# The squares for the last layer's MLP norms in the buffers of the MLP's inner products, and the decode step as a stream of its own beside the first stage

## The chip, the cores and the metric

The kernel runs on one core of one Trainium2 chip. The metric is the device time of one execution in microseconds (us); smaller is better. Times come in runs of a few executions each, of which the median is given.

## The reference, cut to what matters

One inference step of a hybrid decoder with two layers, in float32: 1024 prompt tokens with 16 learned tokens ahead of them, and 8 decode tokens that carry their own states. Width 1024, MLP width 4096. Layer 0 mixes tokens by a convolution; layer 1, the one that matters here, by RWKV-7 time mixing. For the decode tokens that is one step of a recurrence over a 64 x 64 state per head:

```python
def _wkv7_step(S, inp):
    r_t, w_t, k_t, v_t, kk_t, a_t = inp
    sa = jnp.einsum('bhvk,bhk->bhv', S, -kk_t)
    S = (S * w_t[:, :, None, :] + sa[..., None] * (kk_t * a_t)[:, :, None, :]
         + v_t[..., None] * k_t[:, :, None, :])
    y = jnp.einsum('bhvk,bhk->bhv', S, r_t)
    return S, y
...
    yn = ((y - mu) * lax.rsqrt(var + GN_EPS)).reshape(B, T, D_MODEL)
    yn = yn * gn_g.astype(f32) + gn_b.astype(f32)
    bonus = (jnp.sum(r * k * r_k.astype(f32), axis=-1, keepdims=True) * v).reshape(B, T, D_MODEL)
    out = ((yn + bonus).astype(h.dtype) * g) @ w_o
    return out, h[:, -1], S_final.astype(S0.dtype)

def _sqrelu_mlp(h, w_in, w_out):
    return jnp.square(jax.nn.relu(h @ w_in)) @ w_out
...
        h = h + out
        h = h + _sqrelu_mlp(_rmsnorm(h, norm_mlp[i]), w_mlp_in[i], w_mlp_out[i])
```

## The kernel before, in words

Activations lie with the 1024 features on 8 tiles of 128 partitions and the tokens along the free side. A matrix product in float32 is made of three fast passes: weights and activations are each split into a high part and a remainder (`_hi`/`_lo`, `_h`/`_l`), and lines L187, L188 and L189 of `mm3` add high*high, low*high and high*low in PSUM. ScalarE (ACT) writes the high parts, GpSimd (POOL) the weights' remainders in four pieces each (L162), VectorE (DVE) most of the activations' remainders.

The program has three parts: layer 0; the inputs of the time mixing, in four groups of tokens; and the last part, with which this case deals. It takes the tokens in three groups of 328, 352 and 352 (`G2`). For each group `mixer_out` loads the residual `h` (L1484) and the gated mixer output `z`, tile by tile (`zr`, L1488), splits it (`z_h`, `z_l`), multiplies it with `w_o` (`ps_oo`), adds the product to `h` on DVE (L1492), and hands each finished tile to `add`. `add` comes from `square_sums`: ACT squares the tile (L242) and POOL and DVE add the squares of even and odd tiles up (L253); a matmul with a constant (`st_m`, L231) then sums over the partitions for the norm's denominator. `mlp_in` scales `h` into `m_h` and `m_l` (L269, L270), and `mlp` multiplies by `w_in` (`ps_in`), squares, splits into `hh` and `hl` of the pool `hidp` (two buffers of each), and multiplies by `w_out` (`out`), whose product DVE adds to `h` (L340). The first group has an MLP of its own, the first stage; groups two and three share one.

Other work runs beside the first stage, in generators that `filler` advances after each half product and the like: `fill()` is called `points` times in all, and a stream with total `n` is advanced until what it yielded reaches its share of `n`. The streams are:

- `until`: the rest of the prompt's recurrence in chunks of 64 tokens. Its matmuls are small: `A` (128 x 256), then 64 x 64 (`W`, `U`, `S`, `Y`) and 32 x 32 (`gg`, `po`). Four chunks at a time need `inverses`, 30 steps of two DVE instructions each (`tt`, `ni`; L1168, L1169).
- `decode_step`: the recurrence for the decode tokens. Four transposes (`pdd`) go through DRAM (`d_dec`) by DMAs that ACT issues, come back as `dq`, and then 16 rounds of nine DVE instructions each (L1390 to L1398) with a load and a store of `Sdec` on SyncE (SP). It yields 82 in all.
- `norm_gate`: group norm, gate and bonus of up to 128 tokens at a time, in two halves (`ey`, `eq`, `ems`, `ebv`, `egt`, `ez`, and transposes `yn` on TensorE), for the second and third group. It waits by `after` until the recurrence has reached its tokens.

The order of the instructions on each engine is set when the program is built: a scheduler that goes by modelled times takes them by priority, which is the order in which the generators emit them. On the chip each engine runs its list in that order and waits by semaphores. DMAs go out through SP and ACT, over eight semaphore lanes in turn; a DMA is held back until the one before it on its lane is done. Pools lie one above the other in memory, and a tile is written once the earlier users of its bytes are done.

In the kernel before, the squares have a tag of their own with three buffers, so that the fourth square waits for the first to be added:

```python
return square_sums(n, f"m1{g}", lambda k: cur["tmp"].tile([P, cur["n"]], F32, name=f"sq{g}_{k}", tag="sq", bufs=3)[:, :n],
                   (nc.gpsimd, nc.vector))
```

and the decode step stands ahead of the norm gates in one stream of 262.15.

Of the kernel before, what the change touches and what calls it, by code (L numbers as in the profile page):

```python
# [8 lines left out]
F32 = mybir.dt.float32  # L9
# [7 lines left out]
P = 128  # L17
D = 1024
KT = D // P
# [4 lines left out]
NP_TOK = META + SEQ  # L24
# [14 lines left out]
GN = [(lo + i, min(128, n - i)) for lo, n in G2 for i in range(0, n, 128)]  # L39
GN_OF = [[i for i, (lo, n) in enumerate(GN) if a <= lo < a + w] for a, w in G2]  # L40
# [8 lines left out]
def hybrid_step(tc, x_prompt, x_sample, state_conv, state_shift, state_wkv, meta_tokens,  # L49
# [8 lines left out]
    nc = tc.nc  # L58
    ctx = ExitStack()
    with ctx:  # L60
# [48 lines left out]
        for name, ap in vecs:  # L109
            n = ap.shape[0]  # L110
# [11 lines left out]
        cur = {}  # L122
# [151 lines left out]
        def ranked(offset, gen):  # L274

            it = iter(gen)
            while True:
                with tc.high_priority(offset=offset):
                    try:
                        wait = next(it)  # L280
                    except StopIteration:
                        return
                yield wait
# [85 lines left out]
        with ExitStack() as l0:  # L369
# [16 lines left out]
            h = {}  # L386
# [292 lines left out]
            hidp = pool(l0, "hidp0", 2)  # L679
# [463 lines left out]
            carry["tail"] = tail  # L1143


        st = {"done": -1, "ready": -1, "credit": 0.0}
        for name, shape in (("sv", [P, KT, 2, HS]), ("uv", [P, KT, 2, HS])):
            st[name] = wk.tile(shape, F32, name=name)
        for q in range(2):
# [196 lines left out]
        NG = 0  # L1346
# [14 lines left out]
        def decode_step():  # L1361

            with ExitStack() as s:
                dk = pool(s, "dk", 1)
                for q in range(4):
                    pt = bank(f"pdd{q}", "x")
                    for i in range(2):
                        nc.tensor.transpose(pt[:6 * DEC, i * P:(i + 1) * P],
                                            ddec[:, 2 * q + i].rearrange("p i b -> p (i b)"), ident)
                    dst = tt(f"dst{q}", "t2")[:6 * DEC, :256]  # L1370
                    nc.scalar.copy(dst, pt[:6 * DEC, :256])
                    nc.scalar.dma_start(d_dec.rearrange("i b d -> (i b) d")[:, q * 256:(q + 1) * 256], dst)
                    yield 3
                dq = dk.tile([P, 6, HS], F32, name="dq")
                nc.scalar.dma_start(dq, d_dec.rearrange("i b (h c) -> (b h) i c", c=HS))
                yield 6
                sa = dk.tile([P, HS], F32, name="sa")
                yd = dk.tile([P, HS], F32, name="yd")
                HV = HS // 16
                s_in = state_wkv[0].rearrange("b h v k -> (b h) v k")  # L1380
                s_out = o_wkv_sample[0].rearrange("b h v k -> (b h) v k")
                rows = lambda t: t[:, :HV * HS].rearrange("p (v k) -> p v k", k=HS)
                for hv in range(HS // HV):
                    vs = slice(hv * HV, (hv + 1) * HV)
                    S = rows(cur["ey"].tile([P, 4 * P], F32, name=f"Sdec{hv}", tag="ey"))
                    t4 = rows(cur["eq"].tile([P, 4 * P], F32, name=f"t4{hv}", tag="eq"))
                    nc.sync.dma_start(S, s_in[:, vs, :])
                    overv = lambda i: dq[:, i:i + 1, :].broadcast_to([P, HV, HS])
                    overk = lambda t: t.unsqueeze(2).broadcast_to([P, HV, HS])
                    nc.vector.tensor_mul(t4, S, overv(2))  # L1390
                    nc.vector.tensor_reduce(sa[:, vs], t4, axis=AX.X, op=ALU.add)
                    nc.vector.tensor_mul(S, S, overv(0))
                    nc.vector.tensor_mul(t4, overk(sa[:, vs]), overv(3))
                    nc.vector.tensor_add(S, S, t4)
                    nc.vector.tensor_mul(t4, overk(dq[:, 5, vs]), overv(1))
                    nc.vector.tensor_add(S, S, t4)
                    nc.vector.tensor_mul(t4, S, overv(4))
                    nc.vector.tensor_reduce(yd[:, vs], t4, axis=AX.X, op=ALU.add)  # L1398
                    nc.sync.dma_start(s_out[:, vs, :], S)
                    yield 4  # L1400
                nc.scalar.dma_start(d_y[NP_TOK:].rearrange("b (h c) -> (b h) c", c=HS), yd)

        def norm_gate(i):

            lo, n = GN[i]
            KH, NH = KT // 2, KT
            for hf in range(2):
                ps_ = slice(hf * KH, (hf + 1) * KH)
                y, bv, gt, sq = (cur[tag].tile([P, KH * P], F32, name=f"{tag}{i}_{hf}", tag=tag) for tag in ("ey", "ebv", "egt", "eq"))
                nc.sync.dma_start(y[:n], d_y[lo:lo + n, hf * KH * P:(hf + 1) * KH * P])  # L1410
                yield 3
                heads = lambda t: t[:n].rearrange("t (h v) -> t h v", v=HS)
                ms = cur["eq"].tile([P, 2, NH], F32, name=f"ems{i}_{hf}", tag="ems")
                over = lambda j: ms[:n, j].unsqueeze(2).broadcast_to([n, NH, HS])
                nc.vector.tensor_reduce(ms[:n, 0], heads(y), axis=AX.X, op=ALU.add)
                nc.vector.scalar_tensor_tensor(heads(y), over(0), -1.0 / HS, heads(y), op0=ALU.mult, op1=ALU.add)
                nc.scalar.activation(sq[:n], y[:n], AF.Square)
                yield 2
                fm = lambda t: t[:, :KH * n].rearrange("p (k t) -> p k t", k=KH)
                for t, src in ((bv, d_bv), (gt, d_g)):  # L1420
                    nc.sync.dma_start(fm(t), src[:, ps_, lo:lo + n])
                nc.vector.tensor_reduce(ms[:n, 1], heads(sq), axis=AX.X, op=ALU.add)
                nc.scalar.activation(ms[:n, 1], ms[:n, 1], AF.Sqrt, scale=1.0 / HS, bias=eps_t[:n, 2:3])
                nc.vector.reciprocal(ms[:n, 1], ms[:n, 1])
                nc.vector.tensor_mul(heads(y), heads(y), over(1))
                yield 2.5
                pt = bank(f"yn{i}_{hf}", "w")
                for k in range(KH):
                    nc.tensor.transpose(pt[:, k * n:(k + 1) * n], y[:n, k * P:(k + 1) * P], ident[:n, :n])
                z = cur["eq"].tile([P, KH * P], F32, name=f"ez{i}_{hf}", tag="eq")  # L1430
                for k in range(KH):
                    p = hf * KH + k
                    nc.scalar.activation(z[:, k * n:(k + 1) * n], pt[:, k * n:(k + 1) * n], AF.Identity, scale=vec("gn_g", p), bias=vec("gn_b", p))
                w = KH * n
                nc.vector.tensor_add(z[:, :w], z[:, :w], bv[:, :w])
                nc.vector.tensor_mul(z[:, :w], z[:, :w], gt[:, :w])
                nc.sync.dma_start(d_z[:, ps_, lo:lo + n], fm(z))
                yield 2.5


        NEED = [min(-(-(lo + n - META) // HS), NCH - 1) for lo, n in GN]

        def after(last, gen):
            while st["done"] < last:
                yield 1
            yield from gen

        def norm_gates(gs):
            return ranked(NG, chain.from_iterable(after(NEED[g], norm_gate(g)) for g in gs))
        ng0 = norm_gates(GN_OF[0])  # L1450
        PACE = [0, 1.7, 1.7, 0.98]

# [17 lines left out]
        with ExitStack() as l1:  # L1470
# [4 lines left out]
            hidp = pool(l1, "hidp1", 2)  # L1475
            open_ep(l1, 2, "f")
            hl = {}

            NGA, NGB, FA, FB = 262.15, 45.48, 1.57, 40

            def mixer_out(g, residp, actp, fill, add):
                lo, n = G2[g]
# [61 lines left out]
                        wait = next(rec)  # L1544
                    yield wait

            def sums_of(g):
                n = G2[g][1]
                return square_sums(n, f"m1{g}", lambda k: cur["tmp"].tile([P, cur["n"]], F32, name=f"sq{g}_{k}", tag="sq", bufs=3)[:, :n],
                                   (nc.gpsimd, nc.vector))  # L1550

            def group(g, actp, hidp, sums):
                n = G2[g][1]
# [4 lines left out]
            ng2 = norm_gates(GN_OF[2])  # L1558
            fill, rest = filler(2 * KT + MLP_POINTS,
                                ([until(NCH - 1)], FA * CHUNK_WAIT * (NCH - 1 - st["done"])),  # L1560
                                ([decode_step(), norm_gates(GN_OF[1]), ng2], NGA))
            add, sums = sums_of(0)
            mixer_out(0, residp, actp, fill, add)
            mlp(1, [group(0, actp, hidp, sums)], 2, nc.gpsimd, nc.vector, fill)
            for _ in rest:
# [4 lines left out]
            right = dict(side="right")  # L1570
            residp2, actp2, hidp2 = pool(l1, "resid2", 2, **right), pool(l1, "actp2", 1, **right), pool(l1, "hidp2", 2, **right)
            fill, rest = filler(2 * KT, ([ng2], NGB))
            add, sums = sums_of(1)
            mixer_out(1, residp2, actp, fill, add)
            for _ in rest:
                pass
# [1 line left out]
                nc.scalar.dma_start(o_conv_sample[0, q, 0:CB - 1, :], state_conv[0, q, 1:CB, :])  # L1578
            g1 = group(1, actp, hidp, sums)
            fill, rest = filler(2 * KT + MLP2_POINTS, ([ranked(FN, final(0))], FB))  # L1580
            add, sums = sums_of(2)
            mixer_out(2, residp2, actp2, fill, add)
            end = []

# [40 lines left out]
```

## Time and profile before

| | |
|---|---|
| time, median of 3 runs (lowest to highest) | 2852.09 us (2852.02 to 2855.66) |
| the profiled execution: its time, its span | 2859.05 us, 2857.3 us |
| mean granted TensorE clock | 0.961 |
| busy share: TensorE (PE), weight load (PEld), DVE, ACT, POOL | 94%, 90%, 69%, 47%, 60% |
| last part of the program, us from the span's start | about 1856 to the end |
| its first inner product (`ps_in`) | 1916.33 us |

In the views PE is TensorE's matmuls and PEld its weight loads. A row of the timeline has the start in us, the duration in us, the engine, the line, the operation, what it writes and reads, the shapes, and in brackets the idle time before it with what ended that. A row of the waits names who waited for whom, with the sum in us, how often, and the longest. A row of the windows has, for each stretch, the busy us of each engine with the number of instructions, the granted clock as a share of full speed, the DMA engines' busy share and GB/s. A float32 matmul that is not split (`A`, `S`, `Y` and the others of the recurrence) is two records in the trace for one instruction.

### The profile page before, as it was taken

The numbers are of one execution on the slowest core, as the hardware profiler recorded it, in microseconds if no ns is written. First come the engines' busy times: TensorE is split into PE (matmuls) and PEld (weight loads), VectorE is DVE, ScalarE is ACT, GpSimd is POOL, SyncE is SP. The second block draws the span as 40 slices with busy tenths as digits, with TensorE's granted clock in tenths as the row PEclk, the third lists the DMA queues.
The fourth block names the chain that finished last, engine by engine and source line by source line (L and its number), as shares of the span: only waits on it lengthen the run. The fifth ranks groups of instructions, "written<-read, shape, count | busy, mean of one in ns | idle before, by whom it ended". The sixth has DMA issues, their size and how long they took to land. (4 is left out here: it accounts for less than half of the span.)

```text
span 2857.3 us, 54445 instructions
## 1 busy us (share of the span) xinstructions
PE 2677.4 (94%) x20554; PEld 2557.9 (90%) x20554; DVE 1958.0 (69%) x3726; ACT 1345.6 (47%) x2510; POOL 1703.4 (60%) x2295
## 2 busy tenths in 40 slices
PE   8999999999999899878788899979999999999998
PEld 7989999999999898867787788778889999999998
DVE  5999999995455545478896895689656764443444
ACT  5545444543454334565666857634445552222223
POOL 6676877887788775444543554646448783333332
PEclk9999999999999999988899999989999999999999
DMA  6662544454444642777777968856557742222211
GB/s 179 172 184 85 159 135 133 133 179 140 136 129 148 176 138 91 215 194 198 202 215 208 241 165 198 234 156 159 128 161 213 205 128 85 70 72 67 67 60 41
DMA packets 659285, 428.34 MB, mean 150 GB/s; under 512 B 126840, under 2 KB 609208, under 8 KB 659022
## 3 DMA queue, kind: packets, MB, share of 16 engines
q1 hardware_dynamic: 652780, 421.93, 52.6%
q8 instruction: 162, 2.65, 0.4%
q10 hardware_dynamic: 6018, 2.89, 0.4%
q14 instruction: 101, 0.83, 0.1%
q0 software_dynamic: 224, 0.03, 0.0%
HBM read 353.03 MB, written 72.66 MB: 149 GB/s over the span
## 5 line engine op out<-in xcount | busy, mean ns | idle before, releaser
L162 POOL TENSOR_TENSOR wo_lo<-wo_raw,wo_hi 128x256 fp32r<-128x256 f32 x736 | 561.5, 795 | 300.3 <-ACT wo_hi L157 265.5
L162 POOL TENSOR_TENSOR wi_lo<-wi_raw,wi_hi 128x256 fp32r<-128x256 f32 x640 | 490.4, 797 | 275.5 <-ACT wi_hi L157 264.1
L187 PE MATMUL out<-hh,wo_hi 128*128 128x352 f32 (+2 forms) x1536 | 503.5, 328 | 20.1 <-DVE h L340 10.6
L340 DVE TENSOR_TENSOR h<-h,out 128x352 f32<-128x352 f32 (+2 forms) x768 | 386.3, 510 | 197.8 <-PE out L189 196.9
L187 PE MATMUL ps_in<-m_h,wi_hi 128*128 128x352 f32 (+2 forms) x1536 | 497.4, 324 | 12.2 <-ACT m_h L269 11.5
L189 PE MATMUL out<-hl,wo_hi 128*128 128x352 f32 (+2 forms) x1536 | 496.0, 325 | 4.0 <-DVE hl L141 4.0
L188 PE MATMUL out<-hh,wo_lo 128*128 128x352 f32 (+2 forms) x1536 | 499.4, 325 | 0.0
L188 PE MATMUL ps_in<-m_h,wi_lo 128*128 128x352 f32 (+2 forms) x1536 | 496.5, 324 | 0.0
L189 PE MATMUL ps_in<-m_l,wi_hi 128*128 128x352 f32 (+2 forms) x1536 | 496.2, 323 | 0.1
L504 DVE SCALAR_TENSOR_TENSOR cv<-u,wdw,cv 128x352 f32<-128x352 f32 (+2 forms) x720 | 377.3, 575 | 0.7
L157 ACT CAST wi_hi<-wi_raw 128x1024 fp32r<-128x1024 f32 x160 | 168.1, 1050 | 396.9 <-PE out L189 188.4
L157 ACT CAST wo_hi<-wo_raw 128x1024 fp32r<-128x1024 f32 x184 | 192.9, 1049 | 316.8 <-PE out L189 145.6
L187 PEld LDWEIGHTS out<-hh,wo_hi 128*128 128x128 f32 x1536 | 292.6, 191 | 27.5 <-DVE h L340 14.8
L187 PEld LDWEIGHTS ps_in<-m_h,wi_hi 128*128 128x128 f32 x1536 | 290.6, 189 | 14.6 <-ACT m_h L269 11.6
L189 PEld LDWEIGHTS out<-hl,wo_hi 128*128 128x128 f32 x1536 | 291.6, 190 | 6.4 <-DVE hl L141 5.3
L188 PEld LDWEIGHTS out<-hh,wo_lo 128*128 128x128 f32 x1536 | 292.5, 190 | 1.7
L188 PEld LDWEIGHTS ps_in<-m_h,wi_lo 128*128 128x128 f32 x1536 | 290.3, 189 | 2.0
L189 PEld LDWEIGHTS ps_in<-m_l,wi_hi 128*128 128x128 f32 x1536 | 289.9, 189 | 1.9 <-DVE m_l L270 0.5
L327 DVE SCALAR_TENSOR_TENSOR r<-ps_in,rs_m 128x352 f32<-128x352 f32 (+2 forms) x192 | 98.6, 516 | 232.7 <-PE ps_in L189 228.9
L141 DVE TENSOR_TENSOR hl<-s,hh 128x352 fp32r<-128x352 f32 (+2 forms) x192 | 144.5, 754 | 109.9 <-ACT hh L140 109.8
L329 ACT ACTIVATE s<-r 128x352 f32<-128x352 f32 (+2 forms) x192 | 93.7, 490 | 130.8 <-DVE r L327 130.3
L162 POOL TENSOR_TENSOR wv_lo<-wv_raw,wv_hi 128x256 fp32r<-128x256 f32 x96 | 82.8, 892 | 24.1 <-ACT wv_hi L157 23.8
(402 smaller groups left out, 6155.5 us busy)
## 6 DMA issues: line engine op xcount, KB each, us to landing
wi_raw<-in_w_mlp_in_dram SPq DMA_DIRECT2D x160, 512.0 KB
wo_raw<-in_w_mlp_out_dram SPq DMA_DIRECT2D x160, 512.0 KB
wr_raw<-in_rwkv_w_r_dram SPq DMA_DIRECT2D x32, 512.0 KB
wk_raw<-in_rwkv_w_k_dram SPq DMA_DIRECT2D x32, 512.0 KB
wv_raw<-in_rwkv_w_v_dram SPq DMA_DIRECT2D x32, 512.0 KB
d_ab<-ab SPq DMA_DIRECT2D x32, 512.0 KB
pg_raw<-in_conv_w_pw_dram SPq DMA_DIRECT2D x24, 512.0 KB
pa_raw<-in_conv_w_pw_dram SPq DMA_DIRECT2D x24, 512.0 KB
```

The lines of the kernel that those rows point to most:

```text
L141: eng_lo.tensor_sub(lo, src, hi.bitcast(F32))
L157: nc.scalar.copy(hi[:, :a * b], raw[:, :a * b])
L162: eng_lo.tensor_sub(lo[:, cs], raw[:, cs], hi[:, cs].bitcast(F32))
L187: nc.tensor.matmul(ps, w[0], act[0], start=first, stop=False)
L188: nc.tensor.matmul(ps, w[1], act[0], start=False, stop=False)
L189: nc.tensor.matmul(ps, w[0], act[1], start=False, stop=last)
L327: nc.vector.scalar_tensor_tensor(r[:, :n], ps[:, :n], 0.0, rs[:, :n], op0=ALU.max, op1=ALU.mult)
L329: nc.scalar.activation(s[:, :n], r[:, :n], AF.Square)
L340: nc.vector.tensor_add(hv[:, 4 * i + m, :], hv[:, 4 * i + m, :], ps[:, :n])
L504: nc.vector.scalar_tensor_tensor(acc[m][:, :n], ug[:, m, j:j + n], wdw[:, m, j:j + 1], acc[m][:, :n], op0=ALU.mult, op1=ALU.add)
```

## The change

The squares of one group get their memory from `hidp`, the pool of `hh` and `hl`: four tiles of two squares each, so that eight squares have eight places and the two buffers of each tag are taken in turn. `own=True` lets the first two squares serve as the accumulators instead of two tiles `acc`. The tag `sq` and its three buffers are gone, and with them the place of the pools above it changes.

`decode_step` becomes a stream of its own with a total of 100 beside the first stage; the norm gates have one of 180.15 and begin at once. The one norm gate that reads the decode tokens' output waits until the step has been made (`stepped`).

```diff
-        st = {"done": -1, "ready": -1, "credit": 0.0}
+        st = {"stepped": False, "done": -1, "ready": -1, "credit": 0.0}
...
                 nc.scalar.dma_start(d_y[NP_TOK:].rearrange("b (h c) -> (b h) c", c=HS), yd)
+                st["stepped"] = True
...
-        def after(last, gen):
-            while st["done"] < last:
+        def after(last, gen, dec=False):
+            while st["done"] < last or dec and not st["stepped"]:
                 yield 1
             yield from gen
...
-            return ranked(NG, chain.from_iterable(after(NEED[g], norm_gate(g)) for g in gs))
+            return ranked(NG, chain.from_iterable(after(NEED[g], norm_gate(g), sum(GN[g]) > NP_TOK) for g in gs))
...
-            NGA, NGB, FA, FB = 262.15, 45.48, 1.57, 40
+            NGA, NGB, FA, FB, DD = 180.15, 45.48, 1.57, 40, 100
...
-            def sums_of(g):
+            def sums_of(g, hidp):
+
                 n = G2[g][1]
-                return square_sums(n, f"m1{g}", lambda k: cur["tmp"].tile([P, cur["n"]], F32, name=f"sq{g}_{k}", tag="sq", bufs=3)[:, :n],
-                                   (nc.gpsimd, nc.vector))
+                sqs = [hidp.tile([P, 2, cur["wide"]], F32, name=f"sq{g}_{i}", tag="h" + "hl"[i % 2]) for i in range(KT // 2)]
+                return square_sums(n, f"m1{g}", lambda k: sqs[k // 2][:, k % 2, :n], (nc.gpsimd, nc.vector), True)
...
-                                ([decode_step(), norm_gates(GN_OF[1]), ng2], NGA))
-            add, sums = sums_of(0)
+                                ([decode_step()], DD), ([norm_gates(GN_OF[1]), ng2], NGA))
+            add, sums = sums_of(0, hidp)
...
-            add, sums = sums_of(1)
+            add, sums = sums_of(1, hidp)
...
-            add, sums = sums_of(2)
+            add, sums = sums_of(2, hidp2)
```

The change also moves instructions, since the scheduler places everything anew from the last part's start on. Three places follow, each before and after.

PE, in the output product of the first group (`ps_oo_m` is output tile m; `S` and `Y` are the recurrence's 64 x 64 products). Before:

```order
L189 MATMUL ps_oo_3_22893<-z_l,wo_3_hi 128x328
L1209 MATMUL A_22994<-xa_12564,bk_22873 128x256 x2
L1302 MATMUL S_23026<-uv,bkt_22749 64x64 x16
L1309 MATMUL Y_23043<-sv,xa_12563 64x64 x16
L1312 MATMUL Y_23043<-uv,nr_21795 64x64 x3
```

After, later in the same product:

```order
L187 MATMUL ps_oo_5_23024<-z_h,wo_5_hi 128x328
L1302 MATMUL S_23037<-uv,bkt_22757 64x64
L188 MATMUL ps_oo_5_23024<-z_h,wo_5_lo 128x328
L1302 MATMUL S_23037<-uv,bkt_22757 64x64
L189 MATMUL ps_oo_5_23024<-z_l,wo_5_hi 128x328
```

The small products stood as blocks between the third and the fourth tile of `z`; now they stand singly between the matmuls of `ps_oo_5`, `ps_oo_6` and `ps_oo_7`. Up to the first `ps_in` there are 44 groups of one or a few small products with a large one on either side, where there were 2 (33 of 64 x 64, 11 of 32 x 32); from there to the stage's end there are 96 where there were 79.

ACT, at the stage's start (`no`, `sv` are of the recurrence; `eq`, `ems` of a norm gate). Before:

```order
L140 CAST z_h<-zr_22554 128x328
L1295 COPY uv<-U_22951 64x8x64
L1375 DMA dq<-d_dec 128x6x64
L1215 COPY no_22878<-A_22986 32x64 x2
L1215 COPY no_22878<-A_22994 32x64 x2
L1263 COPY sv<-vt_22881 64x8x64 x2
L1215 COPY no_22878<-A_23100 32x64 x2
L140 CAST z_h<-zr_22558 128x328
```

After:

```order
L140 CAST z_h<-zr_22558 128x328
L1418 ACTIVATE eq_0_22692<-ey_0_22689 128x512
L140 CAST z_h<-zr_22562 128x328
L140 CAST z_h<-zr_22566 128x328
L140 CAST z_h<-zr_22570 128x328
L1424 ACT_TABLE_LOAD
L1424 ACTIVATE ems_0_22784<-ems_0_22784,eps_t 128x8
```

The load of `dq` and the recurrence's copies have left the place between the `z` tiles; a norm gate's squares and root have come in.

ACT, around the squares. Before:

```order
L157 CAST wi_0_3_hi<-wi_0_3_raw 128x1024
L242 ACTIVATE sq_3_22919<-h_0_22542 128x328
L242 ACTIVATE sq_4_22983<-h_0_22542 128x328
L242 ACTIVATE sq_5_23097<-h_0_22542 128x328
L242 ACTIVATE sq_6_23153<-h_0_22542 128x328
L269 ACTIVATE m_h<-h_0_22542,pvec 128x328 x7
```

After:

```order
L157 CAST wi_0_3_hi<-wi_0_3_raw 128x1024
L242 ACTIVATE sq_3_22545<-h_0_22546 128x328
L1255 COPY gg_23192<-gg_23175 32x256 x2
L1271 COPY bkt_23202<-bT_23203 128x512
L269 ACTIVATE m_h<-h_0_22546,pvec 128x328 x7
```

The squares were four in a row ahead of `m_h`; now they are spread over the time in which the tiles of `h` come.

## The prediction

> **What bounds the kernel now.** I read the page first, for the engine that decides.
>
> ```profile
> PE 2677.4 (94%) x20554; PEld 2557.9 (90%) x20554; DVE 1958.0 (69%) x3726; ACT 1345.6 (47%) x2510; POOL 1703.4 (60%) x2295
> ```
>
> PE is busy for 94% of the span, so a change pays by what it does to PE: the time in which PE stands, and the time that its own list takes. Instructions that move on other engines count only where PE waits for them. Next come the windows around the edit, the start of the last part.
>
> ```profile
> 1880.00:1900.00 20.00, 20.00 (x158) 19.47 (x157) 18.04 (x37) 9.38 (x14) 11.60 (x14) 1.00 0.49 118
> 1900.00:1920.00 20.00, 8.38 (x76) 7.58 (x75) 20.00 (x35) 6.92 (x14) 15.28 (x19) 0.66 0.53 155
> 1920.00:1940.00 20.00, 20.00 (x132) 17.08 (x132) 19.84 (x50) 9.32 (x18) 10.21 (x15) 1.00 0.36 105
> ```
>
> The first numbers behind the stretch are PE's busy us and its instructions, the third pair is DVE. PE works 8.38 of 20 us in the middle row while DVE works all 20. The waits of 1850 to 1925 name the chain:
>
> ```profile
> PE ps_in L187 <- ACT m_h L269: 11.5, 1, 11.5
> ...
> ACT sq L242 <- DVE acc_m L253: 10.9, 1, 10.9
> ...
> ACT no L1215 <- DMA ni<-d_n: 7.3, 1, 7.3
> ...
> PE ps_oo L187 <- ACT z_h L140: 7.2, 2, 4.8
> ```
>
> PE waits once, 11.5 us, for `m_h`; ACT, which makes `m_h`, had itself stood 10.9 us in front of a square. (The 7.3 us of ACT ahead of `no` come back in part 2.) The timelines of ACT and DVE show why:
>
> ```profile
> 1903.26 0.84 ACT L242 ACTIVATE sq<-h 128x328 f32<-128x328 f32 x2 [0.92 <-POOL acc_m L253]
> 1914.97 0.84 ACT L242 ACTIVATE sq<-h 128x328 f32<-128x328 f32 x2 [10.87 <-DVE acc_m L253]
> 1915.72 3.31 ACT L269 ACTIVATE m_h<-h,pvec 128x328 fp32r<-128x328 f32 x7
> ...
> 1914.45 0.49 DVE L253 TENSOR_TENSOR acc_m<-sq,sq 128x328 f32<-128x328 f32 x1
> ...
> 1916.84 0.48 DVE L1492 TENSOR_TENSOR h<-h,ps_oo 128x328 f32<-128x328 f32 x1
> ```
>
> The three buffers of the squares are full, the next square waits for DVE's first addition, which stands in DVE's list behind inverses and decode rounds, and seven `m_h` wait behind the square. The last row is DVE's eighth addition to `h`. PE had its last `ps_oo` at 1903.5, and when it goes on it is slow for a while:
>
> ```profile
> 1903.52 0.31 PE L189 MATMUL ps_oo<-z_l,wo_hi 128*128 128x328 f32 x1
> ...
> 1916.33 0.64 PE L187 MATMUL ps_in<-m_h,wi_hi 128*128 128x328 f32 x1 [11.51 <-ACT m_h L269]
> 1916.76 0.48 PE L188 MATMUL ps_in<-m_h,wi_lo 128*128 128x328 f32 x1
> 1917.04 0.48 PE L187 MATMUL ps_in<-m_h,wi_hi 128*128 128x328 f32 x1
> ...
> 1920.22 0.32 PE L188 MATMUL ps_in<-m_h,wi_lo 128*128 128x328 f32 x1
> 1920.37 0.31 PE L189 MATMUL ps_in<-m_l,wi_hi 128*128 128x328 f32 x1
> ```
>
> Starts are 0.28 us apart at first and 0.15 us from 1920.2 on: 3.9 us at about half rate, 1.7 us lost.
>
> **Part 1: squares in `hidp`.** With eight places no square waits for an addition. The instructions are the same in number; the additions write a square in place of `acc`. By the order, the squares come one by one with the tiles of `h`, and seven `m_h` stand behind the seventh; nothing of that waits for DVE's sums. So the 11.5 us and the 1.7 us behind them go: -13.2. What is late next is DVE's eighth addition to `h`. Up to it DVE's list has 105 instructions before and 104 now (31 of the decode step have gone, 18 of the inverses and 12 of a norm gate have come), so DVE is no lighter, and it got there at 1916.8 (the row above). The gain of 13.2 therefore holds only because PE itself arrives no earlier than that, by part 3; it is not added to a gain for DVE.
>
> The buffers of `hh` and `hl` are free when squares take them (the readers are matmuls that PE has behind it) and are free again when the sums over partitions have read them, which the first `hh` waits for anyway through the norm: nothing.
>
> **Part 2: decode step and norm gates.** The four `pdd`, the `dq` and the 16 rounds of decode are the same work, later; the `z` tiles no longer share ACT with the `dq` load. Against that, a norm gate's loads, squares and root come in between them. What PE waits for there:
>
> ```profile
> 1856.49 0.64 PE L187 MATMUL ps_oo<-z_h,wo_hi 128*128 128x328 f32 x1 [4.78 <-ACT z_h L140]
> 1866.35 1.15 PE L1302 MATMUL S<-uv,bkt 128*64 128x64 f32 x32
> 1867.34 1.10 PE L1309 MATMUL Y<-sv,xa 128*64 128x64 f32 x32
> ...
> 1872.38 0.56 PE L1312 MATMUL Y<-uv,nr 128*64 128x64 f32 x10
> 1875.37 0.42 PE L187 MATMUL ps_oo<-z_h,wo_hi 128*128 128x328 f32 x1 [2.43 <-ACT z_h L140]
> ```
>
> Until the fourth `z` tile is there PE does `A`, `S` and `Y`. These now stand behind `ps_oo_4`, so 6.6 us of cover are gone (1866.3 to 1872.9), 7 with the `A` ahead of them. The fourth tile came late because of what SP loaded ahead of it:
>
> ```profile
> 1861.17 1.30 SPq L1484 DMA_DIRECT2D h<-d_h  x1
> 1862.52 2.33 SPq L1387 DMA_DIRECT2D Sdec<-in_state_wkv_dram  x2
> 1864.95 1.61 SPq L1488 DMA_DIRECT2D zr<-d_z  x3
> ...
> h<-d_h SPq DMA_DIRECT2D x1, 1312.0 KB
> ```
>
> In the new order the load of `h` stands ahead of the first `zr`, and three norm gate loads of 256 KB have its place and that of two `Sdec` of 128 KB: 800 KB less, 3 us at the 253 GB/s of this stretch:
>
> ```profile
> 1856.00:1877.00 21.00, 17.08 (x155) 15.51 (x156) 12.14 (x34) 6.14 (x17) 2.23 (x2) 0.83 0.98 253
> ```
>
> I take +4 (7 of lost cover less 3). The ends: -7.2, if all `z` tiles come in time and both waits of the rows above go (4.8 and 2.4); +8, if the norm gate's two ACT instructions and table load, which wait for DVE, hold the later tiles too. The fourth `d_dec` and `dq` now stand on ACT among the first splits of the MLP. `dq` waits for its four stores, and behind it in ACT's list stand a `hh` and the recurrence's `no`. Before, `dq` stood just ahead of the `no` that came 7.3 us late, which I put down to it. Now DMA is less loaded (0.36 in 1920 to 1940 against 0.98 below), and the first `out` comes only after four `ps_in` of 24 matmuls, 14 us: 0, or up to 7 if that cover is gone, and then on top of the dear case below. Later in the stage the decode rounds lie beside matmuls as before, where PE hardly waits for DVE: nothing.
>
> **Part 3: single small products among large ones.** This is what the edit's wording doesn't say and the order does. A block is cheap: `S` above takes 0.99 us for 32 records, two records an instruction, so 0.06 us each; `gg` I put at 0.05. A large matmul costs 0.15 (the rows at 1920). Mixed, both are dear:
>
> ```profile
> 1946.65 0.42 PE L189 MATMUL out<-hl,wo_hi 128*128 128x328 f32 x1
> 1947.00 0.33 PE L1312 MATMUL Y<-uv,nr 128*64 128x64 f32 x2
> 1947.26 0.41 PE L187 MATMUL out<-hh,wo_hi 128*128 128x328 f32 x1
> ...
> 1951.03 0.24 PE L1247 MATMUL gg<-x,no 32*32 32x32 f32 x2
> 1951.20 0.41 PE L189 MATMUL out<-hl,wo_hi 128*128 128x328 f32 x1
> 1951.55 0.24 PE L1247 MATMUL gg<-x,no 32*32 32x32 f32 x2
> ...
> 1955.70 0.31 PE L1247 MATMUL gg<-x,no 32*32 32x32 f32 x2
> 1955.94 0.64 PE L188 MATMUL out<-hh,wo_lo 128*128 128x328 f32 x1
> 1956.51 0.31 PE L1247 MATMUL gg<-x,no 32*32 32x32 f32 x2
> ```
>
> From large to large with one `Y` between is 0.61 us in place of 0.21: 0.40 more. From `gg` to `gg` is 0.52 in place of 0.20: 0.32 more. The last three rows are the same pattern after 4 us of it: 0.81, so 0.61 more; the granted clock had fallen.
>
> ```profile
> 1950.00:1954.00 4.00, 4.00 (x25) 2.54 (x24) 3.78 (x10) 1.82 (x3) 1.60 (x2) 1.00 1.13 264
> 1954.00:1958.00 4.00, 4.00 (x24) 2.43 (x24) 1.04 (x4) 0.52 (x1) 0.00 (x0) 0.54 0.33 75
> ```
>
> By the order, `ps_oo` now has 44 such groups (33 of 64 x 64, 11 of 32 x 32) where it had 2. At full clock that is 33 x 0.40 + 11 x 0.32 = 16.7, less 0.6 for the two before, 16. At the low clock, 0.61 x 0.81/0.52 = 0.95 for a `Y` pair, 0.74 more, the sum is 33 x 0.74 + 11 x 0.61 = 31. The groups follow each other without a pause, over some 25 us, so the clock should fall as it did after 4 us; it may come back between. I take half of them at each price: +24. The MLP of the stage has 96 groups where it had 79: 17 x 0.33 = +5.5. They are on the path, since PE stands nowhere in 1920 to 1940 and is what the others wait for.
>
> [...]
>
> **The sum.** -13.2 + 4 + 24 + 5.5 = +20.3. The profiled execution took 2859.05 us, 1.75 more than its span and 7.0 more than the median; its counterpart after would be 2879.4. On the median, 2852.1 + 20.3 = 2872.4. A difference under about 0.2%, 5.7 us, can't be told from none.
>
> **The rivals.**
>
> *Pairs at full clock.* If mixing does not lower the clock, the third term is 16: -13.2 + 4 + 16 + 5.5 = 12.3, or 2864. For it: the first 4 us of mixing kept 1.00; against it: the 0.54 behind them.
>
> *Early `z`.* As before, and the `z` waits go too: -13.2 - 7.2 + 16 + 5.5 = 1.1, or 2853. For it: `h` is loaded earlier; against it: the DMA engines are at 0.98 in that stretch whatever the order, and ACT's list has a norm gate between the tiles.
>
> *Dear.* All pairs at the low clock and the `z` tiles held by the norm gate: -13.2 + 8 + 31 + 5.5 = 31, or 2883, and 2890 with the 7 us behind `dq`.
>
> *Faster: the pairs cost nothing in `ps_oo`.* DVE, not PE, sets that product: it is 18.04 and 20.00 busy of 20 us. If PE would stand for DVE's additions anyway, the mixed rows fill standing time, and if DVE's new instructions are so much shorter than the decode rounds' that it reaches the eighth addition where PE's last `ps_oo` was before, the wait still goes: -13.2 + 5.5 = -7.7, or 2844. It decides where DVE's lag behind PE is over the 24 us that the pairs take; before it was 13.3 (PE's last `ps_oo` at 1903.5, the addition at 1916.8), which speaks against it.
>
> **How the numbers follow.** Forecast 0.50 (its own range 2864 to 2880), full clock 0.14, early `z` 0.12, dear 0.12, faster 0.12. Faster by over 0.2%: 0.12. Within: most of early `z`, 0.10. Slower: the rest, 0.78. The range goes from between early `z` and faster to the end of dear, 2848 to 2890, and leaves out the faster case.
>
> **What would show it.** Right: no wait of PE for `m_h` of over 3 us and none of ACT for `acc_m` or a square's sum; 40 or more starts in `ps_oo` 0.5 to 1 us apart with `S`, `Y` or `gg` between; a granted clock well under 1 in the 30 us before the first `ps_in`; that `ps_in` near 1916.3 - 11.5 + 4 + 24 = 1933. Wrong: a first `ps_in` before 1916 (early `z`, faster), a clock near 1 through the mixed rows (full clock), or PE waiting there for DVE's `h` (faster).

## The result, and the profile after

The changed kernel takes 2890.8 us (median of four runs) where before takes 2853.9 beside it: a ratio of 1.0107, 95% interval 1.0088 to 1.0126. On 2852.1 that is 30.5 us more, 2882.6; 20.3 and 2872.4 had been forecast. (The medians themselves are 36.9 apart, which would be 2889.0, at the end of the range of 2848 to 2890.) The profiled execution grew by 31.6 us, from a span of 2857.3 to 2888.9. Its page has this line for the engines:

```profile
PE 2713.1 (94%) x20554; PEld 2578.4 (89%) x20554; DVE 1956.0 (68%) x3726; ACT 1345.5 (47%) x2510; POOL 1701.9 (59%) x2295
```

PE has the same 20554 instructions and is busy 35.7 us longer, its weight loads (PEld) 20.5 us; DVE, ACT and POOL are not. So the same products cost more. The same three windows as before:

```profile
1880.00:1900.00 20.00, 20.00 (x126) 15.36 (x124) 19.60 (x33) 8.84 (x20) 19.68 (x24) 1.00 0.58 164
1900.00:1920.00 20.00, 20.00 (x111) 12.57 (x111) 10.75 (x29) 5.46 (x12) 6.93 (x9) 0.88 0.56 130
1920.00:1940.00 20.00, 20.00 (x138) 15.33 (x137) 10.34 (x15) 8.94 (x19) 7.37 (x10) 0.93 0.28 77
```

PE no longer stands in the middle row, and DVE, which was full there, is at 10.75. Of the waits of 1850 to 1925 that on `m_h` is gone, that on `z_h` has grown, and DVE now waits for PE:

```profile
DVE h L1493 <- PE ps_oo L189: 12.7, 4, 10.0
...
PE ps_oo L187 <- ACT z_h L140: 11.4, 2, 7.5
```

PE's timeline shows the wait for the fourth `z` tile, the mixed rows at two prices, and the first `ps_in` without a wait:

```profile
1868.78 0.64 PE L187 MATMUL ps_oo<-z_h,wo_hi 128*128 128x328 f32 x1 [7.54 <-ACT z_h L140]
...
1908.18 0.33 PE L1312 MATMUL Y<-uv,nr 128*64 128x64 f32 x2
1908.44 0.41 PE L189 MATMUL ps_oo<-z_l,wo_hi 128*128 128x328 f32 x1
1908.79 0.33 PE L1312 MATMUL Y<-uv,nr 128*64 128x64 f32 x2
...
1915.91 0.31 PE L1247 MATMUL gg<-x,no 32*32 32x32 f32 x2
1916.16 0.64 PE L187 MATMUL ps_oo<-z_h,wo_hi 128*128 128x328 f32 x1
1916.73 0.31 PE L1247 MATMUL gg<-x,no 32*32 32x32 f32 x2
...
1926.17 0.42 PE L187 MATMUL ps_in<-m_h,wi_hi 128*128 128x328 f32 x1
```

From `Y` to `Y` is 0.61 us, the full-clock price; from `gg` to `gg` 0.82, the low one. The windows divide in the same way:

```profile
1880.00:1912.00 32.00, 32.00 (x191) 22.96 (x189) 29.34 (x57) 11.12 (x26) 23.84 (x28) 1.00 0.54 140
1912.00:1924.00 12.00, 12.00 (x68) 8.83 (x67) 1.44 (x5) 4.44 (x10) 2.77 (x4) 0.72 0.56 154
1956.00:1972.00 16.00, 16.00 (x92) 10.12 (x90) 7.81 (x16) 6.58 (x13) 6.08 (x6) 1.00 0.40 109
1972.00:1984.00 12.00, 12.00 (x58) 8.95 (x57) 1.82 (x4) 2.36 (x4) 2.79 (x4) 0.57 0.23 45
```

In a row 128*64 is the tile shape of the product; the large ones have 128*128. While `S` and `Y` (128*64) stand among the large products the granted clock stays at 1.00; in the two stretches where `gg` (32*32) follows it is 0.72 and 0.57.

To place the 31.6 us I walk through PE's rows in both traces, from each start to the next, and part the time into standing and work. "ps_oo" runs from the first `ps_oo` to the first `ps_in`, "MLP" from there to the next group's first `ps_oo`.

| | first ps_oo | ps_oo: standing | ps_oo: work | first ps_in | MLP: standing | MLP: work | end of MLP |
|---|---|---|---|---|---|---|---|
| before | 1856.5 | 14.9 | 44.9 | 1916.3 | 5.8 | 354.3 | 2276.4 |
| after | 1854.3 | 7.5 | 64.4 | 1926.2 | 14.2 | 363.9 | 2304.2 |

So -2.2 ahead of it, -7.4 of standing and +19.5 of work in `ps_oo`, +8.4 of standing and +9.6 of work in the MLP, and 3.8 behind it that I didn't follow.

### The profile page after: what moved, and what is told of

It reads as the page before. It is cut to its first block, busy times and chain, and to the rows that moved or that the text cites. A ratio compares the mean times of both kernels' runs of the same rounds, so it can differ in the third digit from the quotient of the medians.

```text
span 2888.9 us, 54418 instructions
## 1 busy us (share of the span) xinstructions
PE 2713.1 (94%) x20554; PEld 2578.4 (89%) x20554; DVE 1956.0 (68%) x3726; ACT 1345.5 (47%) x2510; POOL 1701.9 (59%) x2295
## 4 chain that ended last, share of the span: by engine, by line
PE 34%; DVE 6%; POOL 6%; issue 3%; DMA 2%; ACT 1%; SPq 0%; DVEq 0%; POOLq 0%; ACTq 0%
PE ps_in L187 4%; PE ps_in L189 4%; PE ps_in L188 4%; PE out L187 3%; PE out L188 3%; PE out L189 3%; POOL wo_lo L162 3%; POOL wi_lo L162 2%; PE A L1209 2%; DVE tt L1168 1%; PE ps_oo L187 1%; PE ps_oo L188 1%; DVE ni L1169 1%; PE ps_oo L189 1%; DVE mx L813 1%
## 5 line engine op out<-in xcount | busy, mean ns | idle before, releaser
L157 ACT CAST wo_hi<-wo_raw 128x1024 fp32r<-128x1024 f32 x184 | 193.0, 1049 | 318.2 <-PE out L189 156.6
L140 ACT CAST hh<-s 128x352 fp32r<-128x352 f32 (+2 forms) x192 | 92.2, 482 | 6.6 <-DMA d_dec<-dst 0.8
```

The source lines that it names most:

```text
L140: nc.scalar.copy(hi, src)
L157: nc.scalar.copy(hi[:, :a * b], raw[:, :a * b])
```

## The experiments

Changes of tile shape (64x64, 32x32, all others) are counted in PE's order, in `ps_oo` and in the MLP of this stage: before 52 and 253, after 133 and 292. The count for `ps_oo` begins ahead of its first product; from that product on, the traces hold 15 in before and 98 in after. Before itself had medians of 2857.2 to 2862.9 beside these kernels, so a time that is held against an expectation is the ratio on 2852.1.

**One part at a time.** The first kernel has the new `sums_of` alone, the second the new streams alone:

```diff
 # squares_only: before, with
-            def sums_of(g):
+            def sums_of(g, hidp):
...
 # stream_only: before, with
-                                ([decode_step(), norm_gates(GN_OF[1]), ng2], NGA))
+                                ([decode_step()], DD), ([norm_gates(GN_OF[1]), ng2], NGA))
```

> The squares in memory of hidp, the decode step left in one stream with the norm gates as before. By the order ps_oo then has 21 groups of small products between two large ones (11 of 64x64, 10 of 32x32) where before has 2 and after 44, and the first MLP 111 where before has 81 and after 98. Mixed products as the cost: the 11.5 us wait for m_h goes and 1.7 behind it; 21 groups at 0.40 and 0.32 are 7.6, up to 13 if the clock falls; 30 more groups in the MLP at 0.33 to 0.6 are 10 to 18. Sum +4 to +18: 2858 to 2872. Rival, the decode stream as the cost: the wait goes and nothing is paid, 2841 to 2845. Rival, the squares' place as the cost: as after, 2885 or more.

> The decode step in a stream of its own as in after, the squares in their three buffers as before. By the order the mixed groups are those of after: 44 in ps_oo, 99 in the first MLP. Mixed products as the cost: PE reaches its last ps_oo some 20 us later than before, so the wait for m_h is mostly hidden under that, and the time is that of after within 8 us: 2883 to 2899. Rival, the squares' place as the cost: as before or below, 2840 to 2856. Rival, both parts pay about half: near 2870.

Measured 1.0061 (1.0047 to 1.0076) and 1.0157 (1.0138 to 1.0176), 17 and 45 us, near the upper ends of the ranges for mixed products. Both parts cost by themselves, and together less than the sum. In squares_only the wait for `m_h` is gone, yet its first `ps_in` starts at 1915.3, 1.0 us sooner than before, and the MLP works 12.4 us longer (315 changes of shape). ACT's timeline says what `m_h` now follows:

```profile
1909.27 0.48 ACT L242 ACTIVATE sq<-h 128x328 f32<-128x328 f32 x1 [6.23 <-DVE h L1492]
...
1911.48 3.33 ACT L269 ACTIVATE m_h<-h,pvec 128x328 fp32r<-128x328 f32 x7
```

The square waited for DVE's addition to `h` instead of its addition of squares. stream_only, at 2896.9, is dearer than after. Its PE timeline has a stop in the mixed rows, and its windows stay at 0.50 behind it:

```profile
1898.26 0.22 PE L1309 MATMUL Y<-sv,xa 128*64 128x64 f32 x1
1900.51 1.11 PE L1209 MATMUL A<-xa,bk 128*128 128x256 f32 x4 [2.03 <-DVE nr L1217]
...
1902.76 0.48 PE L1309 MATMUL Y<-sv,xa 128*64 128x64 f32 x2
1903.16 0.64 PE L188 MATMUL ps_oo<-z_h,wo_lo 128*128 128x328 f32 x1
1903.73 0.48 PE L1309 MATMUL Y<-sv,xa 128*64 128x64 f32 x2
```

```profile
1904.00:1936.00 32.00, 32.00 (x120) 19.09 (x119) 6.80 (x21) 5.55 (x12) 5.03 (x7) 0.50 0.33 91
1940.00:1956.00 16.00, 16.00 (x116) 11.10 (x114) 9.80 (x14) 7.40 (x14) 6.72 (x10) 1.00 0.28 67
```

A `Y` group, from large to large, takes 0.97 us here. The output product has as many such groups as in after; it worked 64.4 us there and works 76.3 us here.

**The products in blocks.** The loops that issue the small products get a raised priority, in this stage only, so that a block that has begun is laid down whole; nothing else is edited:

```diff
+                with tc.high_priority(offset=1000) if st["block"] else ExitStack():
-                for p in range(KT):
+                  for p in range(KT):
...
+            st["block"] = 1000
             fill, rest = filler(2 * KT + MLP_POINTS,
```

after_blocks has it on all of `gg`, `po`, `W`, `U`, `S`, `Y`; after_blocks64 on the last four; after_blocks32 on the first two.

> After, with the small products of the recurrence of this stage (gg, po, W, U, S, Y) raised in priority as blocks, so that a block once begun stays together. By the order ps_oo has 7 mixed groups instead of 44, the first MLP 17 instead of 98; DVE's and ACT's work is the same work. Mixed products as the cost: 37 x 0.38 = 14 in ps_oo and 81 x 0.35 = 28 in the MLP go, and some of the low clock, 42 to 55 less than after, of which PE may give back up to 13 in a wait for h or m_h at the first ps_in: 2836 to 2862. Rival, decode rounds and norm gates on DVE and ACT as the cost: within 10 us of after, 2880 to 2900.

> After, with only the 64x64 products (W, U, S, Y) of this stage raised as blocks; gg and po (32x32) are left to the order. By the order ps_oo has 13 mixed groups (8 of gg), the first MLP 37 (28 of gg and po). If a mixed group costs what the rows show (0.40 for 64x64) without regard to the clock: 31 x 0.38 + 61 x 0.38 = 35 less than after, 2856. If the low clock hangs on the 32x32 groups alone, the windows with gg between large products still fall to half rate, and those with Y were at 1.00 already, so no clock is won: 2850 to 2862. If it hangs on any mixing, the clock is won too: 2835 to 2850.

> After, with only gg and po (32x32) raised as blocks; the 64x64 products stay mixed (70 changes of shape in ps_oo, 239 in the MLP, where after has 83 and 168). If the granted clock falls through 32x32 among large products only: it stays near 1.00 from the fourth z tile to the first ps_in and through the first 60 us of the MLP, and the time is 2868 to 2880. If 64x64 groups lower it too, or keep it low after a stop of PE (as in stream_only, 0.50 for 36 us): windows at 0.5 stand among the Y and W groups, and the time is 2880 to 2900.

Measured 1.0004 (0.9993 to 1.0015), 0.9986 (0.9973 to 0.9999) and 1.0077 (1.0062 to 1.0092). All that the change cost, and a little more, goes when the small products stand in blocks. DVE and ACT keep their work, though the scheduler places it anew; the rival with that work as the cost falls. (2848.1 for after_blocks64 lies at the border of its ranges and says nothing on the clock.) after_blocks with more blocks is no faster than after_blocks64: raised by the same amount, `W` and `po` alternated with each other (159 changes between 64x64 and 32x32), and that is paid too. From `W` to `W` is 0.43 us:

```profile
1950.55 0.33 PE L1279 MATMUL W<-sv,xa 128*64 128x64 f32 x2
1950.81 0.24 PE L1248 MATMUL po<-p,gg 32*32 32x32 f32 x2
1950.98 0.33 PE L1279 MATMUL W<-sv,xa 128*64 128x64 f32 x2
```

after_blocks32 separates the kinds. With 32x32 in blocks and 64x64 still mixed (309 changes; of after, the expectation counts those to and from 64x64 alone, 83 and 168 of 133 and 292) the clock holds up to 2000, but for one stretch:

```profile
1872.00:1912.00 40.00, 40.00 (x290) 32.38 (x289) 35.92 (x73) 18.32 (x39) 25.41 (x29) 1.00 0.44 116
1912.00:1932.00 20.00, 20.00 (x159) 15.00 (x157) 14.97 (x27) 11.12 (x24) 11.66 (x18) 1.00 0.67 160
1936.00:1940.00 4.00, 4.00 (x17) 3.32 (x16) 1.21 (x3) 0.58 (x1) 0.00 (x0) 0.59 0.07 21
1940.00:2000.00 60.00, 60.00 (x519) 46.67 (x518) 29.62 (x56) 24.03 (x48) 25.71 (x30) 1.00 0.54 128
```

In that stretch stand pairs of `U`, whose tile shape is 64*64:

```profile
1936.05 0.41 PE L189 MATMUL ps_in<-m_l,wi_hi 128*128 128x328 f32 x1
1936.40 0.32 PE L1294 MATMUL U<-w,p 64*64 64x64 f32 x2
1936.65 0.59 PE L187 MATMUL ps_in<-m_h,wi_hi 128*128 128x328 f32 x1
1937.18 0.47 PE L1294 MATMUL U<-w,p 64*64 64x64 f32 x2
```

The time is 2874.1, inside the range for a clock that falls through 32x32 only; by the median, 2881.5, it would be just outside, and the windows decide. The clock was the smaller part of the cost: the mixing itself is paid at 1.00 too, and 22.0 of the 30.5 us are left here.

**The four corners in blocks.** The 32x32 loops are now raised by 200 and the 64x64 loops by 2000, so that the two kinds don't alternate. With that edit on each of the four kernels, what the change does apart from the mixing is left.

```diff
 # in quads (gg, po)
-                with tc.high_priority(offset=1000) if st["block"] else ExitStack():
+                with tc.high_priority(offset=200) if st["block"] else ExitStack():
 # at W, U, S, Y
-            with tc.high_priority(offset=1000) if st["block"] else ExitStack():
+            with tc.high_priority(offset=2000) if st["block"] else ExitStack():
```

> After, with W, U, S, Y (64x64) raised as blocks and gg, po (32x32) raised by another amount, so that the two kinds don't alternate with each other as they did in after_blocks (159 changes between 64x64 and 32x32 in this stage, now 7). Changes of tile shape in the stage by the order: 91, where after has 425 and after_blocks64 144. Mixed products as the cost: about 8 to 12 less than after_blocks64, unless PE's standing time in the MLP (20.6 us in after_blocks64) takes it: 2842 to 2856. Rival, that the blocks gain by what they do to the other engines and not by fewer changes: no better than after_blocks, 2856 to 2864.

> The squares in hidp, the decode step left with the norm gates, and the small products of this stage as the two kinds of block. Changes of tile shape: 113 in the stage, where squares_only has 409. Mixed products as the cost: the wait for m_h is gone and little is paid for it: 296/2 groups at 0.2 to 0.33 less than squares_only, 2828 to 2846, under both kernels. Rival, DVE as the bound once the products stand in blocks: PE waits in front of the first ps_in for h or m_h by up to 13, 2846 to 2856.

> Before, with the small products of this stage as the two kinds of block: 118 changes of tile shape, where before has 305. Squares and decode step as before, so ACT's wait for acc_m and PE's for m_h should stay. Mixed products as the cost: 187/2 groups at 0.2 to 0.33 are 19 to 31, less up to 12 of new standing time: 2826 to 2850. Against squares_blocks2 it tells what the squares' place is worth without the mixing: 8 to 13 if the wait stays, 0 if the order has moved it.

> The decode step in a stream of its own, the squares in their three buffers, and the small products as the two kinds of block (89 changes of tile shape in the stage; stream_only has 427). It is the fourth corner: before, squares and after with blocks took 0.9897, 0.9922 and 0.9914 of before. If the 45 us that stream_only cost were the mixed products and the half clock behind them, nothing of it is left: 2825 to 2842. Rival, that the late decode step or the z tiles cost by themselves, and squares in hidp only hid it in after: 2846 or more. Squares' place under a late decode step: this minus after_blocks2, between -8 and +8.

| | as it was | in blocks | changes, ps_oo + MLP | MLP: work | first ps_in |
|---|---|---|---|---|---|
| before | 1 | 0.9897 (0.9884 to 0.9909) | 52+253 → 39+79 | 354.3 → 315.8 | 1916.3 → 1908.7 |
| squares | 1.0061 | 0.9922 (0.9908 to 0.9936) | 94+315 → 30+83 | 366.7 → 318.2 | 1915.3 → 1913.2 |
| stream | 1.0157 | 0.9905 (0.9892 to 0.9918) | 131+296 → 28+61 | 364.4 → 310.2 | 1943.0 → 1916.4 |
| after | 1.0107 | 0.9914 (0.9900 to 0.9928) | 133+292 → 30+61 | 363.9 → 310.7 | 1926.2 → 1912.0 |

The four are 1.6% apart as they were and 0.25% in blocks. The MLP's work falls by 38.5 us over 174 changes, 48.5 over 232, 54.2 over 235 and 53.2 over 231: 0.21 to 0.23 us each, so 0.42 to 0.46 a group, the low clock included. In `ps_oo` the work falls to 49.4 us in after and 49.3 in stream, by 15.0 and 27.0; counted from the first `ps_oo` on, 81 changes have gone in each (98 to 17, 96 to 15): 0.19 and, with the half clock, 0.33 each.

All four beat both kernels. after_blocks2, at 2827.6, and before_blocks2, at 2822.7, gained more than their ranges allowed; stream_blocks2, at 2825.0, lies at the lower end of its own, and the rivals (a gain by way of the other engines, a late decode step that costs by itself) fall. What is left of the change is nothing to gain: after in blocks is at 0.9914, before in blocks at 0.9897, and their intervals overlap. The squares' new place alone had been put at a gain of 8 to 13 or at nothing; squares_blocks2 is 7 us slower than before_blocks2, with intervals that just touch.

And the wait for `m_h` is not tied to where the squares lie. squares_blocks2, with its squares in `hidp`, has the longest one of all, and before_blocks2, with three buffers, a short one. (The wait was the sign of the rival of squares_blocks2; its time, 2829.9, is inside the range without it.) The first fence is the timeline of squares_blocks2 (DVE, ACT, PE), the second that of PE in before_blocks2:

```profile
1885.86 12.23 DVE L1396 TENSOR_TENSOR t<-Sdec,dq 128x256 f32<-128x256 f32 x1
...
1900.88 0.48 ACT L242 ACTIVATE sq<-h 128x328 f32<-128x328 f32 x1 [13.18 <-DVE h L1498]
...
1913.18 0.64 PE L187 MATMUL ps_in<-m_h,wi_hi 128*128 128x328 f32 x1 [14.19 <-ACT m_h L269]
```

```profile
1908.67 0.64 PE L187 MATMUL ps_in<-m_h,wi_hi 128*128 128x328 f32 x1 [3.87 <-ACT m_h L269]
```

**How late the decode rounds come.** The pace `DD` of after_blocks2 is changed from 100 to 262 (sooner) and to 60 (later).

```diff
-            NGA, NGB, FA, FB, DD = 180.15, 45.48, 1.57, 40, 100
+            NGA, NGB, FA, FB, DD = 180.15, 45.48, 1.57, 40, 262
```

> after_blocks2 with the decode stream's pace at 262 in place of 100, so that its 16 rounds come sooner and not among the last additions of the MLP (86 changes of tile shape, after_blocks2 has 91). If the late rounds on DVE are what PE waits for at 2110 to 2240 (r and h, 9 us in after_blocks2): 2824 to 2830. If PE's waits there have another cause: as after_blocks2, 2829 to 2838.

> after_blocks2 with the decode stream's pace at 60 in place of 100: its rounds come later still. Changes of tile shape 94, after_blocks2 has 91. At 262 the kernel took 0.9966 of before, at 100 0.9914. If DVE's decode rounds are dear only beside the recurrence (up to 2090) and cheap behind it, 60 is as good as 100 or better by some us: 2826 to 2836. If they are then waited for behind it, in PE's waits for r and h at 2110 to 2300 and in the norm gates that now follow the decode step: 2838 to 2850.

At 262: 0.9966 (0.9954 to 0.9979), slower by 15 us where I had expected a gain. At 60: 0.9906 (0.9883 to 0.9929), as at 100. The windows of 1990 to 2110, in the kernel with 262 and in after_blocks2, show where it goes:

```profile
1990.00:2110.00 120.00, 102.46 (x956) 96.15 (x957) 100.79 (x219) 50.58 (x99) 70.04 (x86) 0.93 0.59 156
```

```profile
1990.00:2110.00 120.00, 111.73 (x1345) 104.46 (x1343) 94.99 (x198) 57.64 (x121) 69.95 (x84) 1.00 0.66 178
```

Beside the recurrence DVE is what PE waits for (of 17.8 us of waits in the kernel with 262, 14.7 are for DVE), so PE stands 17.5 of 120 us in place of 8.3, and the granted clock is 0.93 in place of 1.00. Over the whole MLP PE stands 26.4 us in place of 20.4 and works 318.1 in place of 310.7.

**Blocks in the whole program.** before_blocks2, with the loops raised from the start.

```diff
-            with tc.high_priority(offset=2000) if st["block"] else ExitStack():
+            with tc.high_priority(offset=2000):
```

> before_blocks2 with the small products raised as blocks in the whole program, not in the last part's first stage alone. By the order the parts ahead of it have 207 changes of tile shape where they had 224, so little is to be had there: 17/2 groups at 0.33 are 3 us. The stage itself has 109 changes, before_blocks2 118. 2822 to 2831; if raised products keep the mixers' PE from its large ones, 2831 to 2845.

Measured 0.9929 (0.9915 to 0.9942), some 9 us slower than before_blocks2: its first `ps_oo` comes at 1860.7 in place of 1851.9. The mixers have little to win, and what they lost I didn't follow.

## Why the prediction was right, and where its sizes were off

The sign and the cause held: the time went into PE's own list, by small products among large ones, and blocks take all of it away. 2882.6 is inside the range, but 10 us over the forecast and over the likeliest case's own 2864 to 2880. By terms:

**-13.2, the wait for `m_h`.** The wait is gone in after, as forecast, but not by the squares' new place. The prediction had said that the gain holds only because PE comes late; the runs show that this is nearly all of it. stream_only, with the old buffers, has no such wait either, squares_blocks2 has 14.2 us of it, and squares_only reached `ps_in` just 1.0 us sooner. What `m_h` follows in these kernels is DVE's seventh addition to `h` (1908.75 in squares_only, 1911.06 in squares_blocks2, 1907.11 in before_blocks2), since seven `m_h` stand behind the seventh square. In before that addition came at 1911.92, less than 3 us ahead of the addition of squares at 1914.45 that ACT waited for. Had PE come as early as before, with DVE no lighter, less than 3 us was to be won; the prediction went by the eighth addition:

```profile
1911.92 0.48 DVE L1492 TENSOR_TENSOR h<-h,ps_oo 128x328 f32<-128x328 f32 x1
```

**+4, the `z` tiles.** The two waits were 3.9 and 7.5 us, 11.4 in all, against 7.2: +4.2 of standing. That the lost cover would show there held; the first wait didn't grow.

**+24, the groups in `ps_oo`.** Measured +19.5 (work from 44.9 to 64.4). The step that failed is "half of them at each price". The 33 groups of `S` and `Y` and the first six of `gg` ran at the full clock, the other five of `gg` at the low one: 33 x 0.40 + 6 x 0.32 + 5 x 0.61 - 0.6 = 17.6, and about 1 us more for the plain rows at half rate behind them, up to 1922.0. I had taken the fall of the clock, seen in the trace before behind `gg`, for a property of any mixing. This term lay between the forecast and the rival at full clock (16). stream_only shows that the dear price of a group is real as well: 0.97 us a `Y` group, where 0.95 had been worked out, and it came behind a stop of 2.03 us. Its total, 76.3 - 44.9 = 31.4, equals the dear sum of 31 by luck: its eleven `S` groups ahead of the stop ran at the full clock, and plain rows at half rate made up for them.

**+5.5, the MLP.** Measured +18.0, the largest miss. 9.6 is work: 39 changes more at 0.23, the price found by the blocks, would be 9.0, where I had taken 17 groups at 0.33, about that of a `gg` pair at full clock. 8.4 is standing, in the step that put the late decode rounds at nothing. DVE, in the windows from 2150 of before and of after:

```profile
2150.00:2200.00 50.00, 50.00 (x335) 49.74 (x335) 32.39 (x60) 25.17 (x43) 42.53 (x55) 1.00 0.70 204
2200.00:2250.00 50.00, 46.99 (x310) 45.89 (x309) 35.01 (x61) 26.61 (x47) 40.21 (x49) 1.00 0.66 194
```

```profile
2150.00:2200.00 50.00, 45.81 (x314) 44.66 (x315) 42.38 (x81) 22.65 (x37) 35.13 (x43) 0.97 0.78 241
2200.00:2250.00 50.00, 45.43 (x281) 43.57 (x280) 45.26 (x88) 19.40 (x28) 38.38 (x47) 0.97 0.54 163
```

It has 20.2 us more to do there, and PE stands 5.8 us longer in these two windows. That this standing is the rounds' net price isn't shown: brought forward in after_blocks2_dd262 they cost more. The misses in `ps_oo` (-4.5) and in the MLP (+12.5) have opposite signs, so the total is nearer than its terms.

**The other signs.** The first `ps_in` was forecast near 1933 and came at 1926.2; a low clock in the 30 us ahead of it was there for 6.8 of them only, 1915.2 to 1922.0. The rival "dear" had the right total, 31, by other parts: its `z` term and its clock didn't occur. "Early `z`" was half right, since the fourth tile's products did start 6.6 us sooner (1868.8 against 1875.4). "Faster" fell: DVE waited for PE.

## What to carry to other kernels

Before costing an edit in a kernel whose order a scheduler lays down, count in that order how often the tile shape changes on the bound engine; here a change cost 0.2 to 0.3 us, and taking 231 of them out of one MLP was worth 53 us, where the edit was about 13. If products of another tile shape stand singly among large ones, raise each kind as a block, and by different amounts, before any other tuning. A wait that an edit removes is only won if what stands next behind it is early; look at that row first.

## What the runs showed of the hardware

**The clock and what is mixed.** Pairs of 128*64 among large products kept 1.00 from their first, at 1888, to 1912; pairs of 32*32 lost it 2.8 us after they began (1912.4 to 1915.2 in after), the next ones, from 1930.8, only at 1939.1, and pairs of 64*64 (`U`) some 8 us after theirs (1928.2 to 1936.7 in after_blocks32), without a stop of PE. In all fourteen traces the granted clock changes only at borders that lie 3.41 us apart, and these falls lie at such borders. In after:

```profile
1908.38:1911.79 3.41, 3.41 (x18) 2.07 (x16) 1.69 (x5) 0.23 (x1) 0.73 (x2) 1.00 0.42 103
1911.79:1915.21 3.42, 3.42 (x31) 2.19 (x30) 1.01 (x4) 2.92 (x5) 0.75 (x2) 1.00 0.34 59
1915.21:1918.62 3.41, 3.41 (x15) 1.95 (x15) 0.00 (x0) 0.00 (x0) 2.02 (x3) 0.50 0.95 273
```

The first of these stretches is full of `Y` pairs, the second of `gg` pairs, and the clock falls behind the second. Counted over 1840 to 2310 us of the fourteen traces, stretches at full clock with less than 0.15 us of standing, eight or more changes of shape and one kind of small product: the low clock followed on none of 41 with 128*64, on 4 of 9 with 64*64 and on 16 of 21 with 32*32. In after_blocks2, where nearly nothing is mixed, it was 1.00 from 1908 to 2032, with 5 us of standing in short stops:

```profile
1908.00:2032.00 124.00, 118.90 (x1375) 109.61 (x1374) 97.09 (x209) 69.58 (x147) 72.05 (x86) 1.00 0.71 178
```

The clock also fell behind stretches in which PE stood for a part of the time only: of 7780 stretches of the traces that hold 128*128 products alone or nothing, ahead of 2800 us and at full clock, the low clock followed on all with more than 1.92 us of standing and on none with less than 1.44. Why it falls behind mixed rows in which PE doesn't stand, no run shows.

**A low clock that lasted through mixed rows.** In stream_only it stayed at 0.50 from 1904 to 1936, though PE never stood, and was 1.00 again from 1940 to 1956, behind the plain large products that begin at 1936.0. The stop of 2.03 us ahead of it is above the 1.92 of the count. In after, too, the clock fell at 2212.2 behind 1.9 us of standing among plain rows, but there it was back 3.4 us later. Behind the stop of 2.03 us a `Y` group among large products cost 0.76 us in place of 0.40; it is one instance, and it wasn't repeated by design.

**Small against small costs too.** 64x64 and 32x32 in turn cost 0.43 us a pair in after_blocks, where 0.11 is the estimate for two blocks (0.06 for an `S`, 0.05 for a `gg`: 1912.4 in after has six `gg` in 0.31 us).

**One DVE row of 12.23 us** (squares_blocks2, above) takes 0.41 in the next round, and the additions to `h` stood behind it. POOL's rows beside it begin and end with it:

```profile
1885.85 5.56 POOL L162 TENSOR_TENSOR wo_lo<-wo_raw,wo_hi 128x256 fp32r<-128x256 f32 x8
...
1895.01 2.80 POOL L162 TENSOR_TENSOR wi_lo<-wi_raw,wi_hi 128x256 fp32r<-128x256 f32 x4
```

Whether they held it wasn't tried.
